# A hybrid attention and recurrence block on one Trainium2 core: the opening in a new order, casts on GpSimd, one output row stored in halves

## The chip, the cores and the metric

The kernel runs on one core of one Trainium2 chip. The metric is the device time of one execution in microseconds (us), as a median over runs. A core has five engines, each with its own in-order queue of instructions: TensorE (PE; its weight loads are shown apart, as PEld), VectorE (DVE), ScalarE (ACT), GpSimd (POOL) and SyncE (SP), which here only issues DMAs. An engine waits at an instruction until what this instruction needs is done, and everything behind it in its queue waits with it.

## The reference, cut to what matters

One decoder layer on x of 1024 tokens by 1024 channels: a conditioned RMSNorm gives h; one large projection gives queries, keys, values, gates and the recurrence's input; windowed attention and a gated linear recurrence follow; two projections are merged, a last projection is gated and added to x, and a final RMSNorm ends it. The change touches only the beginning and the last rows:

```python
mod = c @ w_ada[l] + b_ada[l]
shift, scale, gate = jnp.split(mod, 3, axis=-1)
h = rmsnorm(x, norm_g[l]) * (1.0 + scale[:, None, :]) + shift[:, None, :]
proj = h @ w_in[l]
...
x = x + gate[:, None, :] * (merged @ w_out[l])
return rmsnorm(x, final_g)
```

All is float32. The kernel keeps that precision with products of split operands: each operand is a high part (its value rounded to the matmul's format, `hh` for h and `wh` for a weight) and a low part (the rest, `hl` and `wl`), and a product is the sum of three matmuls, high by high ("h"), low weight by high ("w") and high weight by low ("l").

## The kernel before

**The opening** (to about 68 us) is one hand-written order: a manual schedule fixes, for all five engines, the order in which the code issues instructions.

- `x` comes in eight tiles of 128 tokens (`xt`). For each tile ScalarE squares and sums (`square`), VectorE makes mean and epsilon (`mean`), ScalarE the square root (`root`), and VectorE the reciprocal and the scaling of the tile (`scaled`); for the tiles in `DIAG` VectorE makes only a diagonal matrix, and the scaling happens in the transposition. `flip(i)` transposes tile i on TensorE into four PSUM banks, in two sets that change by pairs of tiles; `out_of(j, p, engine)` evicts bank p of pair j into `xT`, which holds channels by tokens, one row block `kc` (0 to 7) for each 128 channels.
- The condition: `c` is broadcast to all partitions by a matmul (`c_bc`). `modulate(kc)` makes, by two products with accumulation on VectorE, the shift and the scale of the 128 channels of kc from two 512 KB loads of `w_ss`; `scales_of(kc)` finishes them with two small ScalarE instructions. The shift of kc 0 alone comes from a matrix-vector product on TensorE.
- `hi_parts(kc)` makes h's high part on ScalarE (for kc below 4 in two halves of 512 tokens) and then h itself in place (the affine); `lo_parts(kc)` makes the low part on VectorE.
- Four chunks of the large projection are done in the opening (`starts`, numbers 0 to 3). Each chunk's weights come in two halves of 256 KB: half 0 serves kc 0 to 3, half 1 kc 4 to 7. `cast_s(c, i)` makes the high part of half i of chunk c, on ScalarE or GpSimd, and `rest_s(c, i)` the low part on VectorE. `first(kc, terms, chunks)` issues the products of one kc; `chunks(kc)` all three terms, chunk after chunk. There are 192 of them, each 128x128 by 128x512.
- GpSimd also makes the rope angles, a generator of 36 small steps (`angles`), of which `turn(n)` issues the next n. ScalarE's sine (L526) reads the result `trn`; it stands between `chunks(3)` and the shift and scale of kc 5, ahead of the casts of half 1 of chunks 1 to 3.
- Behind this, still in the written order: low parts 5 to 7 and `differences(0)` and `make_operands(0)` on VectorE, and on TensorE `chunks(5)`, then kc 6 and 7 of chunks 0 and 1 (L1605 to L1612).

SP issues all loads of the opening in the order of the code: the tiles of x, the parameters, halves 0 of chunks 2 and 3, `w_ss` for kc 0, halves 0 of chunks 0 and 1, `w_ss` for kc 1 and 2, halves 1 of chunks 0 and 1, and so on.

**The middle** (to about 880 us) runs on TensorE without a pause: Strassen-like products (L709), gates, attention and projections, with the other engines beside them. The change doesn't touch it.

**The end** writes the output in eight rows of 128 tokens by 1024. For rows 6 and 7 the right and the left half are finished by different engines (L1965 by ScalarE, L1969 by VectorE for row 6). Row 6 is stored with one DMA of 512 KB on SP's queue, row 7 with two of 256 KB on SP's and ScalarE's.

Of the kernel before, what the change touches and what calls it, by code (L numbers as in the profile page):

```python
# [12 lines left out]
F32 = mybir.dt.float32  # L13
# [4 lines left out]
AF = mybir.ActivationFunctionType  # L18
ALU = mybir.AluOpType
# [3 lines left out]
P = 128  # L23
S = 1024
D = 1024
# [29 lines left out]
def tile_hybrid_block(ctx, tc, x, pk, rows, posr, posi, c_row, w_ss, w_gate, w_main, w_v,  # L55
# [8 lines left out]
    def f32(ap):  # L64
        return ap.bitcast(F32)
# [24 lines left out]
    def pcol(base, i):  # L90
        return pk_t[:, base + i:base + i + 1]
# [99 lines left out]
    with ExitStack() as st:  # L191
# [14 lines left out]
            xt.append(t)  # L206
        dma(pk_t[:], pk)

        def load_ss(kc):
            for a in (0, 1):  # L210
# [10 lines left out]
        def cast_s(c, i, eng=A):  # L221
            sw[c][i] = slot()
            if eng is G:
                G.tensor_copy(sw[c][i][0][:], raw[c, i])
# [22 lines left out]

        one_row = sp.tile([1, P], F32, name="one_row")
        warm = sp.tile([P, 1], F32, name="warm")
        V.memset(one_row[:], 1.0)  # L250
        zero = rbig[:, :HALF]
        V.memset(zero, 0.0)

# [110 lines left out]
        def square(i):  # L364
            A.activation(junk_t[:].bitcast(BF16), xt[i][:], AF.Square, accum_out=ss[:, i:i + 1])

        def mean(i):
            V.tensor_scalar(out=rr[:, i:i + 1], in0=ss[:, i:i + 1], scalar1=1.0 / D, scalar2=EPS,
                            op0=ALU.mult, op1=ALU.add)

        def root(i):
            A.activation(rr[:, i:i + 1], rr[:, i:i + 1], AF.Sqrt)

        def scaled(i):
            r1 = rr[:, i:i + 1]
            V.reciprocal(r1, r1)
            if i not in DIAG:
                V.tensor_scalar(out=xt[i][:], in0=xt[i][:], scalar1=r1, scalar2=None,
                                op0=ALU.mult)
# [7 lines left out]
        banks = [bk, starts[0] + starts[1]]  # L387

        def flip(i):
            for kc in range(KC):  # L390
                c0 = kc // 4 * 256 + i % 2 * P
                o = banks[i // 2 % 2][kc % 4][:, c0:c0 + P]
                x_ = xt[i][:, kc * P:(kc + 1) * P]
                if i not in DIAG:
                    T.transpose(o, x_, ident[:])
                else:
                    T.matmul(o, x_, dg[i][:], start=True, stop=True)

        def out_of(j, p, eng):
            src = banks[j % 2][p].rearrange("p (a t) -> p a t", a=2)  # L400
            dst = xall[p][:, :, j * 256:(j + 1) * 256]
            if eng is A:
                A.copy(dst, src)
            else:
                V.tensor_copy(dst, src)

        def hi_parts(kc, between=lambda: None):
            kw = dict(scale=gsc[:, kc:kc + 1], bias=shf[:, kc:kc + 1])
            if kc < 4:
                for hf in range(2):  # L410
                    A.activation(hh[kc][hf], xT[kc][:, SL[hf]], AF.Identity, **kw)
            else:
                A.activation(full[kc][0], xT[kc], AF.Identity, **kw)
            between()
            A.activation(xT[kc], xT[kc], AF.Identity, **kw)

        angle = angles()
# [7 lines left out]
        late = {1: [lambda: V.tensor_copy(c_bc[:, SL[0]], psc[0]),  # L425
                    lambda: V.tensor_copy(c_bc[:, SL[1]], psc[1])],
                3: [lambda: out_of(0, 0, V), lambda: out_of(0, 1, V)],
                4: [lambda: out_of(0, 2, V), lambda: out_of(0, 3, A)],
                5: [lambda: out_of(1, 0, V), lambda: out_of(1, 1, V)],
                6: [lambda: out_of(1, 2, A), lambda: out_of(1, 3, A),  # L430
                    lambda: V.scalar_tensor_tensor(
                    out=bng[:], in0=pk_t[:, PK_BSC:PK_BSC + 8], scalar=1.0,
                    in1=pk_t[:, PK_NG:PK_NG + 8], op0=ALU.add, op1=ALU.mult)]}
        for i in range(8):
            square(i)
            mean(i)
            if i:
                root(i - 1)
                scaled(i - 1)
                if i < 6:  # L440
                    turn(3)
                flip(i - 1)
            for f in late.get(i, ()):
                f()
        root(7)
        scaled(7)
        for p in range(4):
            out_of(2, p, A)
        flip(7)
        for k in range(KC):  # L450
            T.matmul(bk[0][:, 0:1], wada[0, 0][:, k * P:(k + 1) * P], pcol(PK_C, k),
                     start=(k == 0), stop=(k == KC - 1))
        for i in range(KEEP_BUSY):
            T.matmul(bk[1], zero[:, 0:P], zero, start=True, stop=True)
# [12 lines left out]
        csn = sp.tile([P, 3, 64], F32, name="csn")  # L467

        def lo_parts(kc):
            if kc < 4:  # L470
                for hf in range(2):
                    V.tensor_tensor(out=hl[kc][hf], in0=xT[kc][:, SL[hf]],
                                    in1=f32(hh[kc][hf]), op=ALU.subtract)
            else:
                V.tensor_tensor(out=full[kc][1], in0=xT[kc], in1=f32(full[kc][0]),
                                op=ALU.subtract)

        def first(kc, terms, cs=range(N_ST)):
            for c in cs:
                h, l = sw[c][kc // 4]  # L480
                c0 = (kc % 4) * P
                for t_ in terms:
                    ww, xh = {"h": (h, hh), "w": (l, hh), "l": (h, hl)}[t_]
                    for hf in range(2):
                        T.matmul(starts[c][hf], ww[:, c0:c0 + P], xh[kc][hf],  # L485
                                 start=(kc == 0 and t_ == "h"), stop=(kc == KC - 1 and t_ == "l"))

# [1 line left out]
            for c in cs:  # L489
                first(kc, terms, (c,))  # L490

        for t_ in "hw":
            first(0, t_, (2, 3, 0))
        scales_of(1)

        def more():
            out_of(3, 2, A)
            out_of(3, 3, A)
        hi_parts(1, more)
        rest_s(1, 0)  # L500
        for t_ in "hw":
            first(1, t_, (2, 3, 0))
        for t_ in "hw":
            for kc in range(2):
                first(kc, t_, (1,))
        lo_parts(0)
# [12 lines left out]
        first(2, "wl")  # L519
        modulate(4)  # L520
        scales_of(4)
# [1431 lines left out]
    def square_d(sl, acc):  # L1953
# [9 lines left out]
    r6 = fs[:, 6, 3:4]  # L1963
    V.reciprocal(r6, fs[:, 6, 2:3])
    A.activation(xo[6][:, RIGHT], xo[6][:, RIGHT], AF.Copy, scale=r6)  # L1965
    gemm(end, A22, wt4, 3, cols=c2)
    add_to(7, c2, end)
    square_d(c2, f[:, 1:2])
    V.scalar_tensor_tensor(out=xo[6][:, LEFT], in0=xo[6][:, LEFT], scalar=r6,  # L1969
                           in1=fg_bc[:, LEFT], op0=ALU.mult, op1=ALU.mult)  # L1970
# [37 lines left out]
def arrange(inputs):  # L2008
# [21 lines left out]
    a["w_ss"][:128] = w_ada[:, :128].reshape(8, 128, 128).transpose(1, 0, 2).reshape(128, 1024)  # L2030
# [26 lines left out]
```

## Time and profile before

| what | value |
|---|---|
| median of 3 runs | 908.18 us (907.96 to 909.19) |
| the profiled execution | 907.33 us |
| its span, first to last instruction | 905.5 us |
| mean granted TensorE clock | 0.998 |
| VectorE, ScalarE, GpSimd busy | 79%, 63%, 13% |
| DMA | 180.74 MB, mean 200 GB/s |

The profiled execution takes 907.33 us, of which 905.5 are the span; 1.8 us lie around it. The median is 0.85 us above it. In the profile's rows, times are us from the span's start. A timeline row gives start, duration, engine, line, operation, what is written and read, how many instructions are merged, and in brackets the idle time before it and what ended it. Line numbers are those of the kernel before; a helper that records an operation gives its own line, so that all DMAs stand at L62.

### The profile page before, as it was taken

Reading aid. Unit: us, or ns where it says so; the run is one execution under the profiler, and the core shown is the slowest. Engines: PE = TensorE matmul, PEld = TensorE weight load, DVE = VectorE, ACT = ScalarE, POOL = GpSimd, SP = SyncE. Lnnn points to the kernel's source line nnn. Section 1 sums busy time; section 2 is a strip of 40 time slices with the busy share of each in tenths; the row PEclk is TensorE's granted clock in tenths of the full one; section 3 lists DMA queues with packets and bytes.
Section 4 is the critical chain, followed back from the end, with each engine's and each line's share of the span. In section 5 each row is a group of like instructions: output and inputs, shape, how many; then the busy total and the mean of one; then the engine's idle time right before and its main releaser. Section 6 shows DMA issues by size and latency. Waiting matters only on the chain.

```text
span 905.5 us, 12663 instructions
## 1 busy us (share of the span) xinstructions
PE 894.3 (99%) x4259; PEld 746.1 (82%) x4259; DVE 718.6 (79%) x1073; ACT 567.2 (63%) x1098; POOL 121.1 (13%) x216
## 2 busy tenths in 40 slices
PE   8999999999999999999999999999999999999996
PEld 6789888888888888888888888888888888888885
DVE  6987688978669875987788597999999847569755
ACT  7965554654566855786585884888888732115435
POOL 6520241200000000000000002343433300000000
PEclk9999999999999999999999999999999999999999
DMA  9828489772435354354446367996656289316504
GB/s 356 338 69 285 165 256 321 256 234 95 151 128 182 121 208 135 124 183 163 158 140 214 105 203 248 349 404 208 215 199 207 74 310 363 140 47 234 207 1 186
DMA packets 87205, 180.74 MB, mean 200 GB/s; under 512 B 8626, under 2 KB 29122, under 8 KB 87140
## 3 DMA queue, kind: packets, MB, share of 16 engines
q1 hardware_dynamic: 83056, 167.07, 52.3%
q0 software_dynamic: 3936, 12.59, 4.3%
q8 instruction: 34, 0.56, 0.3%
q14 instruction: 31, 0.25, 0.1%
q10 hardware_dynamic: 148, 0.27, 0.1%
HBM read 121.34 MB, written 58.95 MB: 199 GB/s over the span
## 4 chain that ended last, share of the span: by engine, by line
PE 93%; DVE 4%; ACT 2%; issue 1%; DVEq 0%; ACTq 0%
PE bk L709 48%; PE rp L173 13%; PE out L1861 6%; PE pmain L173 5%; PE pgate L1025 5%; PE s_ps L1330 3%; PE pv L1403 3%; PE pmain L485 2%; PE bk L485 2%; PE pt L1369 1%; PE pmain L1580 1%; PE pmain L1579 1%; PE pmain L1578 1%; ACT jk L1879 1%; DVE xo L1875 1%
## 5 line engine op out<-in xcount | busy, mean ns | idle before, releaser
L709 PE MATMUL bk<-nh,wh 128*128 128x512 f32 x368 | 143.3, 389 | 0.0
L709 PE MATMUL bk<-nl,wh 128*128 128x512 f32 x368 | 143.2, 389 | 0.0
L709 PE MATMUL bk<-nh,wl 128*128 128x512 f32 x368 | 98.4, 389 | 0.0
L111 DVE TENSOR_TENSOR wl<-r,wh 128x512 fp32r<-128x512 f32 x109 | 75.0, 695 | 24.0 <-ACT wh L105 23.7
L105 ACT CAST wh<-r 128x512 fp32r<-128x512 f32 x107 | 65.5, 618 | 31.0 <-PE rp L173 11.1
L709 PEld LDWEIGHTS bk<-nh,wl 128*128 128x128 f32 x368 | 69.1, 188 | 14.4
L709 PEld LDWEIGHTS bk<-nl,wh 128*128 128x128 f32 x368 | 69.1, 188 | 14.2
L709 PEld LDWEIGHTS bk<-nh,wh 128*128 128x128 f32 x368 | 69.1, 188 | 14.2
L709 PE MATMUL bk<-hl,wh 128*128 128x512 f32 x184 | 71.6, 389 | 0.0
L709 PE MATMUL bk<-hh,wh 128*128 128x512 f32 x184 | 71.6, 389 | 0.0
L111 DVE TENSOR_TENSOR wl<-ws,wh 128x512 fp32r<-128x512 f32 x76 | 52.1, 687 | 7.1 <-ACT wh L105 7.0
L62 POOL DMA_DIRECT2D yh_d<-av x1 | 0.6, 567 | 371.3 <-ACT av L1092 371.3
L1355 ACT ACTIVATE p<-p,small 128x129 f32<-128x129 f32 x128 | 50.0, 396 | 0.0
L709 PE MATMUL bk<-hh,wl 128*128 128x512 f32 x184 | 49.2, 389 | 0.0
L105 ACT CAST wh<-ws 128x512 fp32r<-128x512 f32 x76 | 46.0, 614 | 4.3 <-PE bk L709 2.1
L709 PEld LDWEIGHTS bk<-hh,wl 128*128 128x128 f32 x184 | 34.5, 188 | 7.2
L709 PEld LDWEIGHTS bk<-hl,wh 128*128 128x128 f32 x184 | 34.6, 188 | 7.1
L709 PEld LDWEIGHTS bk<-hh,wh 128*128 128x128 f32 x184 | 34.5, 188 | 7.1
L1330 PEld LDWEIGHTS s_ps<-ks,qs 128*128 128x128 f32 x256 | 34.4, 189 | 3.7 <-DVE p L1345 1.1
L1330 PE MATMUL s_ps<-ks,qs 128*128 128x256 f32 (+1 forms) x256 | 35.3, 280 | 0.6 <-DVE p L1345 0.6
L709 PE MATMUL bk<-hha,wh 128*128 128x512 f32 x92 | 35.8, 389 | 0.0
L709 PE MATMUL bk<-hla,wh 128*128 128x512 f32 x92 | 35.8, 389 | 0.0
(378 smaller groups left out, 2289.3 us busy)
## 6 DMA issues: line engine op xcount, KB each, us to landing
r<-w_main SPq DMA_DIRECT2D x100, 256.0 KB, 4.2
wada<-w_ss SPq DMA_DIRECT2D x16, 512.0 KB, 9.0
qs<-q_d SPq DMA_DIRECT2D x16, 512.0 KB, 4.9
wo_d<-wr SPq DMA_DIRECT2D x28, 256.0 KB, 3.0
wo<-wo_d SPq DMA_DIRECT2D x14, 512.0 KB, 5.1
ks<-k_d SPq DMA_DIRECT2D x12, 384.0 KB, 4.3
xt<-x SPq DMA_DIRECT2D x8, 512.0 KB, 7.0
sma_d<-c SPq DMA_DIRECT2D x16, 256.0 KB, 4.4
```

Source lines behind the costliest of these rows:

```text
L105: A.copy(dst[0][:], src)
L111: V.tensor_tensor(out=dst[1][:], in0=src, in1=f32(dst[0][:]), op=ALU.subtract)
L173: mm = T.matmul(ps[hf], ww, xx[kc][hf], start=(kc == 0 and ww is w_h and xx is xh), stop=(kc == KC - 1 and xx is xl))
L485: T.matmul(starts[c][hf], ww[:, c0:c0 + P], xh[kc][hf], start=(kc == 0 and t_ == "h"), stop=(kc == KC - 1 and t_ == "l"))
L709: W["pe"] = T.matmul(ps, ww[:, kc * P:(kc + 1) * P], b[kc][i], start=(first and n == 0), stop=(n == 11), skip_group_check=not first)
L1025: W["pe"] = T.matmul(ps[:, SL[hf]], ww[:, c0:c0 + P], xx_[:, SL[hf]], start=(ic == 0 and i == 0), stop=(ic == 1 and i == 2))
L1330: W["pe"] = T.matmul(o, qs[:, j, qc], ks[:, kb:n % 2 + 2, b, :], start=(b == 0), stop=(b == 1))
L1355: A.activation(px[:, j, :], px[:, j, :], AF.Exp, bias=sm[:, 0, j:j + 1], accum_out=sm[:, 1, j:j + 1])
L1369: W["pe"] = T.transpose(pt[:, j, :], px[:, j, 0:P], ident[:])
L1403: W["pe"] = T.matmul(pv[:], b, m[:].rearrange("p j q -> p (j q)"), start=(i == 0), stop=(i == len(prods) - 1))
L1578: T.matmul(o, hh[kc][th][:, ts_], wh[:, cols], start=(kc == 0), stop=False)
L1861: T.matmul(o, a[k][x_][:, p * P:(p + 1) * P], b[k][y_][:, cols], start=(first and k == 0 and i == 0), stop=(k == 3 and i == 2), skip_group ...
```

## The change

It reorders the opening and splits one store:

- The mean goes into the root: one ScalarE square root with scale 1/D and the epsilon as bias, from the sum of squares; the eight VectorE instructions of `mean` are gone. `DIAG` is 0 and 2 only, so tile 4 is scaled by VectorE. `flip` goes through the kc in the order 0, 4, 1, 5, ..., and tile 5 is flipped twice.
- The matrix-vector product of kc 0 goes; its shift is made by `modulate(0, (0,))` on VectorE, and its `w_ss` half is loaded ahead of the weights of chunks 2 and 3.
- GpSimd makes `bng` and five casts (half 0 of all four chunks, and half 1 of chunk 0, which ScalarE made later), after 17 steps of the angles, and the other 19 steps after them.
- The first products are made by halves of the tokens, over all four chunks; the high-part products of kc 0 and 1 come ahead of their low parts.
- Row 6's right half is stored as soon as it is ready, the left half after it.

```diff
-DIAG = 0, 2, 4
+DIAG = 0, 2
...
+        load_ss(0, (0,))
         for c in (2, 3):
             load_s(c, 0)
-        load_ss(0)
+        load_ss(0, (1,))
...
-            A.activation(shf[:, kc:kc + 1], mods[:, kc:kc + 1] if kc else bk[0][:, 0:1],
-                         AF.Identity, bias=pcol(PK_BSH, kc))
+            A.activation(shf[:, kc:kc + 1], mods[:, kc:kc + 1], AF.Identity,
+                         bias=pcol(PK_BSH, kc))
...
-        def mean(i):
-            V.tensor_scalar(out=rr[:, i:i + 1], in0=ss[:, i:i + 1], scalar1=1.0 / D, scalar2=EPS,
-                            op0=ALU.mult, op1=ALU.add)
         def root(i):
-            A.activation(rr[:, i:i + 1], rr[:, i:i + 1], AF.Sqrt)
+            A.activation(rr[:, i:i + 1], ss[:, i:i + 1], AF.Sqrt, scale=1.0 / D, bias=eps[:])
...
+        norm(0, 1)
+        scaled(0)
+        scaled(1)
+        for hf in range(2):
+            V.tensor_copy(c_bc[:, SL[hf]], psc[hf])
+        flip(0)
+        flip(1)
+        norm(2, 3, 4)
+        scaled(2)
+        scaled(3)
+        evict(0, v=(0, 1, 2), a=(3,))
+        turn(14)
+        flip(2)
+        flip(3)
+        scaled(4)
+        norm(5)
+        evict(1, a=(3,))
+        norm(6)
+        scaled(5)
+        flip(4)
+        flip(5)
+        flip(5)
+        modulate(0, (0,))
+        scaled(6)
+        norm(7)
+        evict(1, v=(0, 1), a=(2,))
         scaled(7)
-        for p in range(4):
-            out_of(2, p, A)
+        evict(2, a=(0, 2, 3, 1))
+        flip(6)
         flip(7)
-        for k in range(KC):
-            T.matmul(bk[0][:, 0:1], wada[0, 0][:, k * P:(k + 1) * P], pcol(PK_C, k),
-                     start=(k == 0), stop=(k == KC - 1))
...
-        for c in (2, 3):
+        for c in (2, 3, 0, 1):
             cast_s(c, 0, G)
-        cast_s(0, 0)
+        cast_s(0, 1, G)
         turn()
         modulate(0, (1,))
-        for p in range(2):
-            out_of(3, p, A)
         scales_of(0)
-        hi_parts(0, lambda: cast_s(1, 0))
-        for c in (2, 3, 0):
-            rest_s(c, 0)
-        modulate(1)
+        rest_s(2, 0)
+        rest_s(3, 0)
...
+        hi_half(0, 0)
+        first(0, "hw", (2, 3), (0,))
+        evict(3, a=(0,), v=(2,))
+        affine_half(0, 0)
+        rest_s(0, 0)
+        rest_s(1, 0)
+        modulate(1, (0,))
+        first(0, "h", (0, 1), (0,))
+        hi_half(0, 1)
+        lo_half(0, 0)
+        modulate(1, (1,))
+        first(0, "h", (2, 3), (1,))
+        first(0, "w", (0, 1), (0,))
+        first(0, "w", (2, 3), (1,))
+        evict(3, a=(1, 3))
+        affine_half(0, 1)
+        first(0, "hw", (0, 1), (1,))
+        first(0, "l", (2, 3, 0, 1), (0,))
         scales_of(1)
...
+        hi_parts(1)
+        lo_half(0, 1)
+        for hf in range(2):
+            first(1, "hw", (2, 3, 0, 1), (hf,))
+        first(0, "l", (2, 3, 0, 1), (1,))
         modulate(2)
         scales_of(2)
         hi_parts(2)
         lo_parts(1)
-        first(0, "l")
         first(1, "l")
         first(2, "h")
         modulate(3)
         scales_of(3)
         hi_parts(3)
         lo_parts(2)
-        cast_s(0, 1)
         first(2, "wl")
...
     A.activation(xo[6][:, RIGHT], xo[6][:, RIGHT], AF.Copy, scale=r6)
+    dma(out[6 * P:7 * P, RIGHT], xo[6][:, RIGHT])
...
-    dma(out[6 * P:7 * P, :], xo[6][:])
+    dma(out[6 * P:7 * P, LEFT], xo[6][:, LEFT])
```

New helpers: `norm` is `square` and `root` of each tile named; `evict(j, a, v)` calls `out_of` for the banks in `a` on ScalarE and then for those in `v` on VectorE; `hi_half`, `affine_half` and `lo_half` are one half (512 tokens) of `hi_parts` and `lo_parts`.

More of the change, by code (lines that the diff above doesn't have):

```diff
@@ L207, in tile_hybrid_block, with load_ss @@
         dma(pk_t[:], pk)
-        def load_ss(kc):
-            for a in (0, 1):
+        def load_ss(kc, which=(0, 1)):
+            for a in which:
                 wa_t = sp.tile([P, D], F32, tag="xt", name="wada", bufs=XT)
@@ L389, in flip @@
         def flip(i):
-            for kc in range(KC):
+            for kc in (0, 4, 1, 5, 2, 6, 3, 7):
                 c0 = kc // 4 * 256 + i % 2 * P
@@ L434, in tile_hybrid_block, with norm, evict @@
[L434 to L445, printed above, removed]
+        def norm(*tiles):
+            for i in tiles:
+                square(i)
+                root(i)
+        def evict(j, **by):
+            for eng, ps in ((A, by.get("a", ())), (V, by.get("v", ()))):
+                for p in ps:
+                    out_of(j, p, eng)
@@ L466, in tile_hybrid_block, with hi_half, affine_half, lo_half @@
-        modulate(1)
+        rest_s(2, 0)
+        rest_s(3, 0)
+        def hi_half(kc, hf):
+            A.activation(hh[kc][hf], xT[kc][:, SL[hf]], AF.Identity, scale=gsc[:, kc:kc + 1],
+                         bias=shf[:, kc:kc + 1])
+        def affine_half(kc, hf):
+            x_ = xT[kc][:, SL[hf]]
+            A.activation(x_, x_, AF.Identity, scale=gsc[:, kc:kc + 1], bias=shf[:, kc:kc + 1])
         csn = sp.tile([P, 3, 64], F32, name="csn")
+        def lo_half(kc, hf):
+            V.tensor_tensor(out=hl[kc][hf], in0=xT[kc][:, SL[hf]], in1=f32(hh[kc][hf]),
+                            op=ALU.subtract)
@@ L471, in lo_parts @@
                 for hf in range(2):
-                    V.tensor_tensor(out=hl[kc][hf], in0=xT[kc][:, SL[hf]],
-                                    in1=f32(hh[kc][hf]), op=ALU.subtract)
+                    lo_half(kc, hf)
             else:
@@ L476, in lo_parts, with first @@
                                 op=ALU.subtract)
-        def first(kc, terms, cs=range(N_ST)):
+        def first(kc, terms, cs=range(N_ST), halves=range(2)):
             for c in cs:
@@ L483, in first @@
                     ww, xh = {"h": (h, hh), "w": (l, hh), "l": (h, hl)}[t_]
-                    for hf in range(2):
+                    for hf in halves:
                         T.matmul(starts[c][hf], ww[:, c0:c0 + P], xh[kc][hf],
```

33 lines of the change are left out of this document (7 added, 26 removed).

## The prediction

> **What bounds the kernel now.** I read the page first, then the waits of PE, then the timelines of the first 70 us engine by engine, and last the end of the span.
>
> ```profile
> span 905.5 us, 12663 instructions
> PE 894.3 (99%) x4259; PEld 746.1 (82%) x4259; DVE 718.6 (79%) x1073; ACT 567.2 (63%) x1098; POOL 121.1 (13%) x216
> PE bk L485 <- ACT hha L411: 0.8, 2, 0.7
> PE s_ps L1330 <- DVE p L1345: 0.6, 1, 0.6
> PE bk L485 <- ACT hhb L411: 0.2, 1, 0.2
> ```
>
> The page says that TensorE is busy for 99% of the span, and PE's waits (total, times, longest) say that after the opening it hardly waits at all. So a time that PE loses or wins in the first 70 us goes through to the end almost one for one.
>
> ```profile
> 23.44 0.47 PE L485 MATMUL bk<-hha,wh 128*128 128x512 f32 x1 [0.68 <-ACT hha L411]
> 27.73 0.50 PE L485 MATMUL bk<-hhb,wh 128*128 128x512 f32 x1 [0.20 <-ACT hhb L411]
> 48.04 0.62 PE L485 MATMUL pmain<-hh,wh 128*128 128x512 f32 x2
> 59.83 0.61 PE L485 MATMUL pmain<-hl,wh 128*128 128x512 f32 x2
> 57.72 5.44 PE pmain L485 x24
> ```
>
> PE's timeline: the four-chunk products start at 23.44 and run without a gap from 27.73. The last row, from the chain that ended last, prices one product at 5.44/24 = 0.227 us. By the order in the code, the product at 48.04 is the first of chunk 1 with kc 4 and needs the cast of that chunk's second half; the one at 59.83 is the first with the low part of kc 7.
>
> **What is moved, and what it costs: GpSimd.** The change puts five weight casts into GpSimd's queue, the fifth being the second half of chunk 0, `cast_s(0, 1, G)`, and behind them `turn()`, the rest of the rope angles. Before, that fifth cast was ScalarE's:
>
> ```profile
> 37.04 0.61 ACT L105 CAST wh<-r 128x512 fp32r<-128x512 f32 x1
> 17.09 1.62 SPq L62 DMA_DIRECT2D r<-w_main  x2
> r<-w_main SPq DMA_DIRECT2D x1, 256.0 KB, 9.8
> 15.17 1.28 POOL L224 CAST wh<-r 128x512 fp32r<-128x512 f32 x2 [0.57 <-DMA r<-w_main]
> 20.45 0.78 POOL L291 TENSOR_SCALAR ra<-sa 128x64 f32<-128x64 f32 x1
> 31.97 1.03 POOL L356 TENSOR_SCALAR trn<-trn 128x128 f32<-128x128 f32 x1
> ```
>
> Its data, r(0,1), are issued at 17.09 and take 9.8 us to land (the third row is the DMA view of that one issue), so they are there at 26.9. The reordering of the loads doesn't change this: one 512 KB load passes two of 256 KB, and every byte ahead of r(0,1) is the same. GpSimd is in order. Its other casts (0.61 us each, from 1.28/2) end soon after their loads, by about 20.3; then it stands still until 26.9, where before it was working through the angles. The generator has 36 steps. Before, 18 were done ahead of the casts, the other 18 ran from the casts' end at 16.45 to 33.00, so 0.92 us each. After, 3 + 14 = 17 are done early and **19 stand behind the fifth cast**.
>
> How long do 19 take? Alone such a step is short, beside VectorE it is not:
>
> ```profile
> 7.40 0.32 POOL L297 TENSOR_TENSOR a<-ang,t 128x64 f32<-128x64 f32 x1
> 22.56 1.28 POOL L291 TENSOR_SCALAR rt<-tt 128x64 f32<-128x64 f32 x1
> 22.22 1.34 DVE L275 SCALAR_TENSOR_TENSOR jk<-wada,c_bc 128x1024 bf16<-128x1024 f32 x1
> 44.03 1.22 DVE L275 SCALAR_TENSOR_TENSOR jk<-wada,c_bc 128x1024 bf16<-128x1024 f32 x1
> L275 DVE SCALAR_TENSOR_TENSOR jk<-wada,c_bc 128x1024 bf16<-128x1024 f32 x10 | 12.4, 1242 | 0.2
> L472 DVE TENSOR_TENSOR hlb<-xT,hhb 128x512 fp32r<-128x512 f32 x3 | 2.3, 774 | 0.0
> L472 DVE TENSOR_TENSOR hla<-xT,hha 128x512 fp32r<-128x512 f32 x3 | 2.1, 688 | 0.1
> L111 DVE TENSOR_TENSOR wl<-r,wh 128x512 fp32r<-128x512 f32 x3 | 2.0, 689 | 0.9 <-ACT wh L105 0.9
> L475 DVE TENSOR_TENSOR hl<-xT,hh 128x1024 fp32r<-128x1024 f32 x1 | 1.2, 1220 | 0.0
> ```
>
> The step at 22.56 ends at 23.84, just behind VectorE's product (22.22 to 23.56). From 20.45 to 33.00 GpSimd makes 13 steps, and VectorE about as many operations: it lets one step in between two of its own. The last five rows are VectorE's groups from 28 to 47 us, 20 operations in 19 us, of the kind that will run there after the change too. The fifth cast, against a running product, ends near 28.4. At the old 0.92 us, 19 steps end at 28.4 + 17.5 = 45.9. At one step per operation they end with the 19th operation behind the cast, the second product of kc 6; that one ended at 45.25 (the row at 44.03). After the change VectorE is some 2 us later there, since modulate(2) can start near 29.0 where it started at 27.04, and a step of GpSimd beside it costs most operations about 0.1 us (1.34 against 1.22): 48.6. Both ends stay in the range; I take **48.0**, nearer the second, since the stretch past 39 us has more long products.
>
> The Trainium skill, page "SBUF — State Buffer", section "Who interferes with whom", says that a VectorE instruction with two SBUF inputs and a GpSimd one that reads SBUF exclude each other, the later one waiting for the whole of the earlier. By that rule the sum takes the later end, 48.6, rather than 45.9; the rows above agree with it (1.28 us beside the product, 0.32 without).
>
> **Who waits for the angles.** ScalarE's sine reads them, and a queue stands behind it:
>
> ```profile
> 40.70 1.28 ACT L526 ACT_TABLE_LOAD   x1
> 41.99 0.31 ACT L526 ACTIVATE csn<-trn 128x128 f32<-128x128 f32 x1
> 45.52 1.65 ACT L105 CAST wh<-r 128x512 fp32r<-128x512 f32 x3
> 46.16 1.90 DVE L111 TENSOR_TENSOR wl<-r,wh 128x512 fp32r<-128x512 f32 x3 [0.90 <-ACT wh L105]
> 57.83 1.22 DVE L475 TENSOR_TENSOR hl<-xT,hh 128x1024 fp32r<-128x1024 f32 x1
> ```
>
> Before, the angles were there 9 us ahead of the sine at 41.99. Behind it on ScalarE: the sine's copy, scale and shift of kc 5, its high part and affine, and the casts of chunks 1 to 3, whose first starts 45.52 - 41.99 = 3.53 us after the sine. VectorE's rests wait for those casts (46.16), and behind them stand the low parts of kc 5 to 7; the last ends at 59.05, 12.89 us after 46.16. PE needs it at 59.83, so this line has 0.78 us to spare now. After: sine at 48.0, first cast at 51.6, rests from 52.2, low part of kc 7 at 65.1. PE, waiting first near 48 for the cast of chunk 1 (about 4 us) and again for that low part (under 1 us), does the old 59.83 product at 65.1: **+5.3 us**. Put as a rule: PE loses (end of the angles - 42.7) us. With 45.9 it is +3.2, with 48.6 +5.9. The opening's own saving doesn't soften this, since the line doesn't run through PE.
>
> **The front.** Off: the 16 matvec passes on PE, three ScalarE casts (37.04's 0.61 us each), eight means on VectorE, one diagonal flip, `bng`. On: modulate(0, shift) on VectorE (1.24 us), a full scaling for tile 4, one more eviction by VectorE, a flip of tile 5 made twice as filler. The root that takes over the mean stays one short instruction on ScalarE, which waits for tiles of x in that stage anyway: nothing. `bng` goes to GpSimd's idle time ahead of the casts: nothing, unless the casts were waited for. On SP one load changes places with two and no issue is added here.
>
> ```profile
> 20.04 1.84 PE L451 MATMUL bk<-pk_t,wada 128*128 128x1 f32 x16
> 23.73 1.23 DVE L275 SCALAR_TENSOR_TENSOR jk<-wada,c_bc 128x1024 bf16<-128x1024 f32 x1 [0.16 <-DMA wada<-w_ss]
> 18.27 0.75 DVE L378 TENSOR_SCALAR xt<-xt,rr 128x1024 f32<-128x1024 f32 x1
> 13.35 0.68 DVE L405 COPY xT<-bk 128x512 f32<-128x512 f32 x1
> ```
>
> VectorE is what paces the new order. From about 15.7 (w_ss(0) lands some 0.6 us after the 15.17 at which GpSimd got the half as large r(2,0) in the same place; scaling 5 is done too): product 1.26, scaling 6 0.9, two evictions 1.2, scaling 7 0.9, product 1.2, and about 0.8 behind GpSimd's casts: 22.0. ScalarE then makes the scale and the first high half, and PE starts near **23.0** (23.44 before). Then two rests, one eviction, two rests, product, low half, product: 6.1 us more, so modulate(1) ends at 28.1, where it ended at 24.96 before. PE has 20 products done by then and waits until 29.3 for kc 1; before, at 29.3, it had done 13 + (29.3 - 27.73)/0.227 = 20. So the new opening wins **nothing** (bounds: 0.9 won if GpSimd costs VectorE nothing; 0.5 lost if it costs twice that). What ends last there is VectorE's product of kc 1, no longer ScalarE.
>
> **The end.** Row 6 goes out in halves.
>
> ```profile
> 898.70 0.72 ACT L1965 ACTIVATE xo<-xo,rbig 128x512 f32<-128x512 f32 x1 [0.23 <-DVE rbig L1964]
> 899.37 0.75 DVE L1969 SCALAR_TENSOR_TENSOR xo<-xo,rbig,fg_bc 128x512 f32<-128x512 f32 x1
> 900.00:900.80 0.80, 0.00 (x0) 0.00 (x0) 0.76 (x3) 0.57 (x1) 0.00 (x0) 1.00 0.00 0
> 902.40:903.20 0.80, 0.00 (x0) 0.00 (x0) 0.00 (x0) 0.00 (x0) 0.00 (x0) 0.71 0.99 394
> ```
>
> The right half is ready at 899.42, the left at 900.12; the DMA engines move nothing until 900.8 (last two columns: share, GB/s), then rows 6 and 7 at up to 394. Half a row, 0.262 MB, takes 0.67 us at that rate and can now go in the idle 0.7 us; SP's one issue more is made while SP waits for the left half: **-0.65** (between 0, if the last landing is bound by latency, and -0.7).
>
> **The sum:** +5.3 - 0.65 = +4.65 us on the profiled execution's 907.33, and 908.18 + 4.65 = **912.8** on the median (the execution lies 0.85 below it). With the bounds +3.2 and +5.9 and the tail's 0: 910.7 to 914.1.
>
> **The rivals.** (1) GpSimd is through in time, and the time doesn't rise. It decides at 42.7: 19 steps in 14.3 us, 0.75 each. For it: alone they take 0.32 to 0.45, and VectorE may have more gaps than I think. Against it: 0.92 before, with the same neighbour. Then only the tail and the front are left: 0 to -0.9 and -0.65, about **907.5**. (2) As (1), and the front also wins more than an us, because products and scalings run free of GpSimd from 20.3 to 26.9: **906.2**. (3) PE's clock falls in the long gap. At the start, after idling, 12 small products take 4.55 us, later four take 1.02, while the granted clock reads 1.00 throughout:
>
> ```profile
> 1.38 4.55 PE L256 MATMUL bk<-rbig 128*128 128x512 bf16 x12 [1.38 <-DVE warm L258]
> 21.74 1.02 PE L454 MATMUL bk<-rbig 128*128 128x512 bf16 x4
> ```
>
> That is 4.55 - 12 x 0.255 = 1.5 us lost. If a gap of 4 us brings this back, the time is 912.8 + 1.5 = **914.3**, partly taken back by the second wait, which shrinks. No gap of that length stands in the trace of before. The Trainium skill, page "TensorE: Matmul & The Clock Gate", section "What's actually happening", speaks of half clock after an idle window of some 3.4 us; by that rule a gap just above it can fall either way.
>
> **Chances.** Forecast 0.60, clock 0.13, in time 0.18, front wins 0.07, others 0.02. A measurement of this kernel can tell about 0.2%, 1.8 us, from no change. Faster 0.08, same 0.18 (906.4 to 910.0), slower 0.74. The forecast's own range is 910.2 to 914.5; to leave out no more than 2 in 10 it has to take in rival (1) and the clock: 907.3 to 915.2.
>
> **What would show it.** After: GpSimd's fifth cast waits for a DMA from about 20 to 26.9; the last `trn` step ends at 46 to 49; ScalarE's sine waits for POOL some 4 us; PE has one gap of 3 to 5 us near 48 before a chunk 1 product with kc 4, released by the cast, and one under 1 us near 65; modulate(1) ends near 28. If `trn` ends before 43, the forecast is wrong and rival (1) holds; if the gap is there but kc 4's products are spaced over 0.3 us, rival (3).

## The result, and the profile after

| | before | after |
|---|---|---|
| median | 908.07 us (6 runs, 907.62 to 909.19) | 912.58 us (6 runs, 910.82 to 913.71) |
| ratio of after to before, 95% interval | | 1.0051 [1.0041, 1.0061] |
| the profiled execution | 907.33 us | 910.82 us |

The changed kernel is 4.5 us slower; 912.8 was forecast. The two profiled executions differ by 3.5 us only: 3.2 in the span and 0.3 around it (1.8 us before, 2.1 after). The rest is taken up further down. First the page of the kernel after:

```profile
span 908.7 us, 12629 instructions
PE 893.3 (98%) x4242; PEld 743.8 (82%) x4243; DVE 720.4 (79%) x1068; ACT 567.2 (62%) x1095; POOL 126.6 (14%) x221
```

Its view of TensorE's waits (total, times, longest, in us):

```profile
PE pmain L394 <- DVE xT L404: 1.5, 1, 1.5
PE pmain L506 <- ACT wh L105: 1.4, 1, 1.4
...
PE s_ps L1358 <- DVE p L1373: 0.9, 2, 0.7
PE bk L506 <- ACT hha L410: 0.7, 1, 0.7
PE pmain L506 <- DVE hl L496: 0.5, 1, 0.5
...
PE pmain L1606 <- DVE c L645: 0.2, 1, 0.2
```

TensorE is busy for 1 us less than before, and the span is 3.2 us longer: the time is lost in waits. The first row is new too, but it stands ahead of the products, in the transpositions (at 18.99), and the first four-chunk product comes no later for it: 23.07 against 23.44. Behind 30 us three waits of the opening are new: for a weight cast (`wh`), for a low part (`hl`), for a rotated piece of chunk 0 (`c`). The timeline of the kernel after shows where they stand and who made them:

```profile
23.07 0.47 PE L506 MATMUL bk<-hha,wh 128*128 128x512 f32 x1 [1.01 <-ACT hha L478]
29.30 0.50 PE L506 MATMUL bk<-hha,wh 128*128 128x512 f32 x1 [0.67 <-ACT hha L410]
46.70 0.62 PE L506 MATMUL pmain<-hh,wh 128*128 128x512 f32 x2
49.61 0.73 PE L506 MATMUL pmain<-hh,wh 128*128 128x512 f32 x2 [1.39 <-ACT wh L105]
62.54 0.73 PE L506 MATMUL pmain<-hl,wh 128*128 128x512 f32 x2 [0.53 <-DVE hl L496]
71.62 0.36 PE L1606 MATMUL pmain<-wh,hha 128*128 128x256 f32 x1 [0.16 <-DVE c L645]
...
25.64 0.62 POOL L224 CAST wh<-r 128x512 fp32r<-128x512 f32 x1 [5.13 <-DMA r<-w_main]
26.34 0.69 POOL L325 TENSOR_SCALAR tmp<-t 128x64 f32<-128x64 f32 x1
44.37 1.03 POOL L359 TENSOR_SCALAR trn<-trn 128x128 f32<-128x128 f32 x1
...
42.05 1.28 ACT L554 ACT_TABLE_LOAD   x1
45.43 0.31 ACT L554 ACTIVATE csn<-trn 128x128 f32<-128x128 f32 x1 [2.10 <-POOL trn L359]
48.96 1.64 ACT L105 CAST wh<-r 128x512 fp32r<-128x512 f32 x3
...
26.72 1.25 DVE L278 SCALAR_TENSOR_TENSOR jk<-wada,c_bc 128x1024 bf16<-128x1024 f32 x1
28.62 1.25 DVE L278 SCALAR_TENSOR_TENSOR jk<-wada,c_bc 128x1024 bf16<-128x1024 f32 x1
49.59 1.90 DVE L111 TENSOR_TENSOR wl<-r,wh 128x512 fp32r<-128x512 f32 x3 [2.08 <-ACT wh L105]
61.27 1.22 DVE L496 TENSOR_TENSOR hl<-xT,hh 128x1024 fp32r<-128x1024 f32 x1
```

Read it from the middle. GpSimd stands for 5.13 us in front of the fifth cast, which waits for its load. Its 19 steps follow, from 26.34 to 45.40, 1.00 us each. ScalarE has loaded the sine's table at 43.33 and waits 2.10 us for `trn`. The casts start 3.53 us behind the sine, as before, VectorE waits 2.08 us for them, and TensorE meets two holes: chunk 1 of kc 4 starts at 49.61, where 48.04 stood before, and the low part of kc 7 at 62.54, where 59.83 stood: +1.57 and then +2.71 us. At 46.70 TensorE was still where the kernel before had it (46.68, the same product in that timeline). The first product of v, next in the timelines of before and after:

```profile
68.44 0.28 PE L1578 MATMUL pmain<-wh,hha 128*128 128x256 f32 x1
```

It comes at 71.62 instead of 68.44, +3.18 us; a further 0.55 comes in at the start of the attention (the wait for `p`), and 0.5 is won at the very end. Sum: 3.2 us of span.

### The profile page after: what moved, and what is told of

It is laid out like the page before. It is cut to its first block, busy times and chain, and to the rows that moved or that the text cites. A ratio compares the mean times of both kernels' runs of the same rounds, so it can differ in the third digit from the quotient of the medians.

```text
span 908.7 us, 12629 instructions
## 1 busy us (share of the span) xinstructions
PE 893.3 (98%) x4242; PEld 743.8 (82%) x4243; DVE 720.4 (79%) x1068; ACT 567.2 (62%) x1095; POOL 126.6 (14%) x221
## 4 chain that ended last, share of the span: by engine, by line
issue 43%; PE 41%; DVE 6%; DMA 4%; ACT 2%; POOL 2%; SPq 0%; DVEq 0%; ACTq 0%; POOLq 0%
PE rp L173 14%; PE bk L737 7%; PE out L1889 6%; PE pmain L173 5%; PE s_ps L1358 3%; PE pv L1431 3%; DMA r<-w_main 2%; PE pt L1397 1%; DMA yl_d<-it 1%; PE pmain L1606 1%; PE pmain L1608 1%; PE pmain L1607 1%; DMA xt<-x 1%; DMA wr<-w_gate 1%; ACT jk L1907 1%
## 5 line engine op out<-in xcount | busy, mean ns | idle before, releaser
L105 ACT CAST wh<-r 128x512 fp32r<-128x512 f32 x104 | 63.6, 617 | 30.3 <-PE rp L173 11.1
```

Of the source, the lines that this page charges most:

```text
L105: A.copy(dst[0][:], src)
```

## The experiments

There are twelve runs, e1 to e13 without an e11; e6 is the changed kernel itself. Medians are compared with runs of the kernel before on the same chip, 907.61 to 908.17 us in the median of each set.

| run | median | ratio to before, 95% interval |
|---|---|---|
| e1, cast back on ScalarE | 909.04 us | 1.0018 [1.0009, 1.0026] |
| e2, cast on GpSimd behind the angles | 908.91 us | 1.0015 [1.0006, 1.0024] |
| e3, before, with that cast ahead of the angles | 911.67 us | 1.0043 [1.0031, 1.0056] |
| e4, before, with the split store | 907.33 us | 0.9994 [0.9985, 1.0003] |
| e5, after, sine behind the casts | 909.11 us | 1.0014 [1.0006, 1.0023] |
| e6, after once more | 912.03 us | 1.0055 [1.0042, 1.0068] |
| e7, e1 with the sine behind the casts | 908.89 us | 1.0008 [1.0000, 1.0017] |
| e8, e1 with the shift of kc 0 on TensorE | 908.95 us | 1.0018 [1.0006, 1.0031] |
| e9, after, with the load issued earlier | 909.13 us | 1.0016 [1.0007, 1.0025] |
| e10, e1 with the low part of kc 7 earlier | 909.18 us | 1.0019 [1.0010, 1.0028] |
| e12, e4 with the mean in the root | 907.42 us | 0.9996 [0.9987, 1.0005] |
| e13, before, products of kc 2 made twice | 909.46 us | 1.0023 [1.0012, 1.0034] |

### Is it the cast that waits ahead of the angles? (e1, e2, e3, e9, e5)

e1 undoes one line of the change, e2 only moves it, e3 makes it alone in the kernel before:

```diff
# e1, on the kernel after
-        cast_s(0, 1, G)
         turn()
...
         lo_parts(2)
+        cast_s(0, 1)
# e2, on the kernel after
-        cast_s(0, 1, G)
         turn()
+        cast_s(0, 1, G)
# e3, on the kernel before
+        cast_s(0, 1, G)
...
-        cast_s(0, 1)
```

> The changed kernel with the second-half cast of chunk 0 back on ScalarE, behind the low part of kc 2. Theory (the cast's wait for its load holds up the angles, the sine, the later casts and so TensorE): GpSimd no longer waits at 25.6, the 19 steps start near 20.5 and end near 40, before ScalarE reaches the sine at 43.3; TensorE has no wait near 48 and no more than 0.9 us near 60; what is left of the change is the front (within 0.5 us of nothing) and the split store (-0.5): 907.0 to 908.3 us. Rival (the loss comes from the new front itself, or from VectorE being slowed by the casts of half 0): the time stays above 910.

> The changed kernel with that cast still on GpSimd, but behind the 19 steps of the angles instead of ahead of them. Theory: the cast comes near 40, its low part is made on VectorE near 41 and needed by TensorE near 47, the sine doesn't wait: within 0.6 us of the kernel with the cast on ScalarE, 907.0 to 908.5. Rival (it is the cast's work on GpSimd that costs, by keeping VectorE off the memory port): it stays over 1 us above that kernel.

> The kernel before with one edit: the second-half cast of chunk 0 moved from ScalarE into GpSimd's queue ahead of the last 18 steps of the angles. Theory: the cast waits for its load until 26.9 and ends near 27.5, 18 steps of 1.0 us end near 45.6, and by the rule of the prediction (loss = end of the angles - 42.7) TensorE loses 2.9 us: 910.3 to 911.8. Rival (the loss belongs to the new front): within 0.5 us of the kernel before.

In e1 and e2 the last step of the angles (L359) ends at 37.57 and 38.35, nobody waits for `trn`, and TensorE's wait for the casts is gone. From the timeline of e1, the last step and the two waits of TensorE's that are left behind 48 us:

```profile
36.54 1.03 POOL L359 TENSOR_SCALAR trn<-trn 128x128 f32<-128x128 f32 x1
...
59.84 0.73 PE L505 MATMUL pmain<-hl,wh 128*128 128x512 f32 x2 [0.55 <-DVE hl L495]
68.92 0.35 PE L1606 MATMUL pmain<-wh,hha 128*128 128x256 f32 x1 [0.17 <-DVE c L645]
```

e2 makes the same cast on the same engine and is as fast as e1: it isn't the work of the cast that costs, but its place. Both are slower than expected, though (909.04 and 908.91, where at most 908.3 and 908.5 were expected); the next section is about that. e3 brings the stall into the kernel before (timeline):

```profile
25.92 0.79 POOL L224 CAST wh<-r 128x512 fp32r<-128x512 f32 x1 [9.97 <-DMA r<-w_main]
44.14 1.03 POOL L356 TENSOR_SCALAR trn<-trn 128x128 f32<-128x128 f32 x1
...
45.21 0.31 ACT L526 ACTIVATE csn<-trn 128x128 f32<-128x128 f32 x1 [3.32 <-POOL trn L356]
...
49.39 0.73 PE L486 MATMUL pmain<-hh,wh 128*128 128x512 f32 x2 [1.35 <-ACT wh L105]
62.33 0.73 PE L486 MATMUL pmain<-hl,wh 128*128 128x512 f32 x2 [0.56 <-DVE hl L476]
71.42 0.36 PE L1578 MATMUL pmain<-wh,hha 128*128 128x256 f32 x1 [0.18 <-DVE c L617]
```

One moved line makes the whole chain of the kernel after: the same waits, the first product of v at +2.98 us, the median at +0.43%. The two runs that follow attack the chain at its other links: e9 lets the data come earlier, and e5 takes away who waits.

```diff
# e9, on the kernel after
+        load_s(0, 1)
         load_ss(1)
         load_ss(2)
-        load_s(0, 1)
# e5, on the kernel after
         chunks(3)
-        (sine, its negated copy and their stores)
...
         for c in range(1, N_ST):
             cast_s(c, 1)
             rest_s(c, 1)
+        (sine, its negated copy and their stores)
```

> Changed kernel, all casts and steps where they are, but the load of the second half of chunk 0 is issued ahead of the loads of w_ss(1) and w_ss(2) instead of behind them (2 MB earlier, about 5 us at the 400 GB/s of that stretch). Theory (GpSimd loses its 5 us standing in front of a cast whose data aren't there): the cast starts at about 20.5 us without a wait, the angles end near 40 to 41 us, the sine doesn't wait, TensorE's wait of 1.4 us for the casts of chunks 1 to 3 goes, and the time is that of the runs without a stall, 908.5 to 909.5 us. Rival (w_ss(1) then lands too late for the product of kc 1 on VectorE, which is due at 24.5 us): the stall goes, but TensorE waits 0.6 us or more longer for kc 1, and the time is 909.6 to 910.5 us.

> Changed kernel, but the sine, its negated copy and its stores are issued behind the casts and rests of chunks 1 to 3 instead of ahead of them; the cast of the second half of chunk 0 stays on GpSimd ahead of the angles. Theory (the angles are late, and cost time only because ScalarE's queue stands behind the sine): GpSimd ends its angles near 45.4 us as in the changed kernel, the casts start near 44 to 45 us instead of 48.96, TensorE's wait for the casts is gone, and the time is that of the two runs without a stall or a little less, 907.3 to 909.3 us. Rival (GpSimd's work of 26 to 45 us itself slows VectorE, or the new front costs the time): 911 us or more.

e9's timeline, then e5's:

```profile
20.75 1.14 POOL L224 CAST wh<-r 128x512 fp32r<-128x512 f32 x1 [1.02 <-DMA r<-w_main]
39.20 0.53 POOL L359 TENSOR_SCALAR trn<-trn 128x128 f32<-128x128 f32 x1
...
42.91 0.31 ACT L554 ACTIVATE csn<-trn 128x128 f32<-128x128 f32 x1
```

```profile
44.86 1.03 POOL L359 TENSOR_SCALAR trn<-trn 128x128 f32<-128x128 f32 x1
...
45.75 1.64 ACT L105 CAST wh<-r 128x512 fp32r<-128x512 f32 x3
47.41 1.28 ACT L562 ACT_TABLE_LOAD   x1
48.71 0.31 ACT L562 ACTIVATE csn<-trn 128x128 f32<-128x128 f32 x1
```

In e9 the cast waits 1.02 instead of 5.13 us, and the sine no longer waits; its rival is there in small, the wait for kc 1 is 0.9 instead of 0.7 us. In e5 the angles are as late as after the change (45.89), but the casts don't stand behind them any more. Both take 909.1 us, as e1 and e2 do. Four different cuts, one time: the stall is the wait of the cast, handed on through GpSimd's queue, the sine and ScalarE's queue, and it costs 912.0 to 912.6 less 909.0, so 3.0 to 3.6 us. e5's rival, that GpSimd's late work costs the time by slowing VectorE, falls: its angles are as late as after the change, and its median is e1's.

### Why do these four take 909 us, and not less than before? (e4, e12, e6)

Without the stall the forecast was about 907.5, and the expectation of e1 was like it; all four come out about 1.5 us above. Is the split store to blame? e4 makes it alone in the kernel before:

```diff
+    dma(out[6 * P:7 * P, RIGHT], xo[6][:, RIGHT])
...
-    dma(out[6 * P:7 * P, :], xo[6][:])
+    dma(out[6 * P:7 * P, LEFT], xo[6][:, LEFT])
```

> The kernel before with row 6 stored in halves and nothing else. Theory: the right half moves in the idle 0.7 us ahead of the left one: 0.4 to 0.7 us faster, 907.4 to 907.7. Rival (the last landing is bound by latency): no difference.

e4's ratio of 0.9994 can't be told from 1. Its span shows the gain nevertheless: from VectorE's last operation on row 6 (899.37 before, 900.45 in e4, 903.10 after) to the span's end (905.5, 906.1, 908.7) it is 6.1 us before and 5.6 in both others. The left half of row 6 in the timeline of the kernel after, then two of its windows (columns: window, length, busy time of PE, PEld, DVE, ACT and POOL, PEclk, DMA share, GB/s):

```profile
903.10 0.75 DVE L1998 SCALAR_TENSOR_TENSOR xo<-xo,rbig,fg_bc 128x512 f32<-128x512 f32 x1
...
903.20:904.00 0.80, 0.00 (x0) 0.00 (x0) 0.76 (x3) 0.33 (x2) 0.00 (x0) 1.00 0.00 0
904.00:904.80 0.80, 0.00 (x0) 0.00 (x0) 0.72 (x1) 0.68 (x1) 0.00 (x0) 1.00 0.92 353
```

The left half of row 6 is ready at 903.85, and from 904.0 on the DMA engines move data, some 0.2 us later; before, nothing moved until 900.8, 0.7 us behind the left half (900.12).

> Kernel before with two edits of the change alone: row 6 stored in halves (907.33 in its own run) and the mean inside the root, which takes eight short operations and a hop between ScalarE and VectorE out of the opening. Theory (VectorE and the hop pace the scalings of the old opening): the first four-chunk product starts 0.2 to 0.5 us earlier, time 906.8 to 907.2 us, the fastest of all. Rival (loads and ScalarE's squares pace them): no change of the opening, 907.2 to 907.7 us.

The mean in the root, the change's other clean part, leaves the old opening as it was: the first product starts at 23.60 in e12, and at 23.29 to 23.94 in the four other profiles of the old opening. The time is the rival's; that loads and squares are what paces this opening is not shown by it.

> The changed kernel once more, on the chip of the next three runs, for a second profile. Theory (the late angles cost all of the loss): about 912.6 us, the end of the angles between 45.0 and 46.0 us, one wait of TensorE of about 1.4 us for a cast of chunks 1 to 3 and one of about 0.5 us for the low part of kc 7. Rival (the surplus of the median over the profiled execution comes from the angles ending later in other executions): the end of the angles moves by more than 1 us between the two profiles, and the time of the profiled execution with it.

The second profile repeats the first: the last step ends at 45.23 (45.40), TensorE's waits are 1.4 and 0.6, the profiled execution takes 910.19 us. So between these two the angles don't wander. That doesn't rule the rival of e6 out, since in both sets the profiled execution is the fastest, 1.8 us below its median, while it is 0.7 below in the kernel before (907.33, 908.07). What the slower executions of the changed kernel lose in addition stands in no trace here; they lose it within their spans (910.0 to 911.6 us, against 908.7).

### The front wins, and VectorE gives it back (e7, e8, e10, e13)

What the runs without a stall lose in the opening can be read from two rows each. Counted from the first four-chunk product, the first product of v comes 45.00, 45.23 and 45.51 us later in the three profiles of the old front without added work (before, e12, e4), and 46.4 to 46.8 in the seven of the new front without the stall: 1.4 us more in the mean. The new front starts its products at 22.75 in the mean of nine profiles against 23.55 in five with the old front. So 0.8 us are won there, and 1.4 are lost behind it.

The candidate was the queue that ends with the low part of kc 7, since TensorE waits 0.55 us for it in e1. It runs over ScalarE and VectorE. e7 relieves ScalarE of the sine, e8 VectorE of one product:

```diff
# e7, on e1: the sine behind the casts, as in e5
# e8, on e1
-        modulate(0, (0,))
...
+        for k in range(KC):
+            T.matmul(bk[0][:, 0:1], wada[0, 0][:, k * P:(k + 1) * P], pcol(PK_C, k),
+                     start=(k == 0), stop=(k == KC - 1))
```

> Changed kernel with the cast of the second half of chunk 0 back on ScalarE (as in the first run, 909.04) and the sine behind the casts of chunks 1 to 3. Theory (without the stall the new front still loses what it won, because the queue of ScalarE and VectorE that ends with the low part of kc 7 has only 0.8 us to spare): taking the sine, its copy and its table load out of that queue brings the low part of kc 7 at least 1 us earlier, TensorE's wait of 0.5 us for it goes, and the time falls by 0.5 to 1.2 us against the first run: 907.8 to 908.6 us. Rival (the front's loss sits ahead of 30 us or behind 70 us): the wait goes, and the time stays within 0.3 us of 909.0.

> Changed kernel with the cast of the second half of chunk 0 back on ScalarE, and the shift of kc 0 made by 16 passes on TensorE again instead of the product on VectorE (1.24 us). Theory (VectorE paces the new front and all of the line behind it): first product and the low part of kc 7 come 0.6 to 1.2 us earlier, time 908.0 to 908.6 us. Rival (loads or ScalarE pace the front): within 0.3 us of the first run's 909.0, or slower by the passes' 0.5 us or so.

Both theories missed. In e7 the casts start 0.7 us earlier than in e1, counted from the first product (46.27 - 22.91 against 46.26 - 22.21), and still the low part of kc 7 ends 37.5 us behind it, where e1 has 37.6. The wait for `hl` stays at 0.6 us, and the median stays too; its ratio is lower than e1's, but the intervals overlap. In e8 the VectorE time taken out ahead of 19 us was idle time in part, VectorE waits 0.82 us for ScalarE at 27.68 instead, and neither the first product (23.06) nor the median improves. What the two traces do show is VectorE's own line: from 19 to 60 us it hardly stops but for ScalarE's casts (0.90 us before, 0.68 in e1), and it begins the products of kc 2 later. In the timelines of the kernel before, of the kernel after and of e1:

```profile
27.04 1.34 DVE L275 SCALAR_TENSOR_TENSOR jk<-wada,c_bc 128x1024 bf16<-128x1024 f32 x1
...
28.62 1.25 DVE L278 SCALAR_TENSOR_TENSOR jk<-wada,c_bc 128x1024 bf16<-128x1024 f32 x1
...
27.75 1.25 DVE L278 SCALAR_TENSOR_TENSOR jk<-wada,c_bc 128x1024 bf16<-128x1024 f32 x1
```

Against the first product that is 3.60 us before and 5.55 and 5.54 in the two others, 1.9 us more; the low part of kc 7 had 0.78 us to spare. e10 takes the wait for this low part away, and e13 delays VectorE in front of kc 2 in the kernel before, by 2.5 us of added work, where nothing else is changed:

```diff
# e10, on e1
     differences(0)
+    lo_parts(7)
     make_operands(0)
     chunks(5)
-    lo_parts(7)
# e13, on the kernel before
         modulate(2)
+        modulate(2)
```

> Changed kernel with the cast of the second half of chunk 0 on ScalarE (the first run, 909.04), and in VectorE's queue the low part of kc 7 ahead of the two operands nl of 2.4 us instead of behind them. Theory (what the new front wins ahead of 30 us is lost because VectorE, which works without a gap from 19 to 60 us, comes 0.7 to 1.4 us later to the low part of kc 7 than before; it isn't ScalarE's queue, as the run with the sine moved showed): TensorE's wait of 0.5 to 0.6 us for that low part goes, the first of the following products comes 0.5 to 0.7 us earlier, and the time is 908.0 to 908.5 us. Rival (the next wait, that of the products of v for the rotated chunk 0, takes it back): the wait for hl goes, that for c grows from 0.2 to 0.7 us, and the time stays at 909.0.

> Kernel before with the two products of kc 2 on VectorE made twice, 2.5 us more of VectorE in front of kc 2 and nothing else. Theory (the line of VectorE from there to the low part of kc 7 is what the opening ends on, with only 0.78 us to spare in the kernel before, so a front that hands it over later loses the surplus, even where TensorE starts earlier): TensorE, without a wait there before, waits near 60 us, 1.7 us in all for the low part of kc 7 and for what stands ahead of it, the first product of v comes 1.7 to 2.2 us later against the first four-chunk product, and the time is 909.3 to 910.0 us. Rival (VectorE's own waits, 0.90 us for the casts among them, take the surplus up): less than 0.8 us, 908.4 us at most.

One of TensorE's waits in e10, and then its timeline in e13:

```profile
PE pmain L1606 <- DVE c L645: 0.9, 1, 0.9
```

```profile
23.50 0.47 PE L485 MATMUL bk<-hha,wh 128*128 128x512 f32 x1 [0.68 <-ACT hha L411]
...
48.52 0.73 PE L485 MATMUL pmain<-hh,wh 128*128 128x512 f32 x2 [0.22 <-ACT wh L105]
61.45 0.73 PE L485 MATMUL pmain<-hl,wh 128*128 128x512 f32 x2 [0.57 <-DVE hl L475]
70.53 0.36 PE L1579 MATMUL pmain<-wh,hha 128*128 128x256 f32 x1 [0.17 <-DVE c L618]
```

In e10 the wait for `hl` is gone, and that for `c`, 9 us further down VectorE's queue, grows from 0.2 to 0.9: its rival held, and the time is e1's. In e13 2.5 us of VectorE work bring the kernel before the two waits of e1, with a third for a cast: the low part of kc 7 is used 1.62 us later than at 59.83, the first product of v comes 47.03 us behind the first four-chunk product (+2.03), and the median rises by 0.23%, to 909.46. The theory held, but for the sum of the listed waits (1.7 us expected, 0.96 found; the last section says why). So in this opening VectorE's line is a second bound close behind TensorE's, with two due points; moving one of them only shows the other.

The opening so explains some 0.6 us (1.4 less 0.8) of the 1.5. Two more places show in the records. One lies at 566 us, at the start of the attention: its third group of scores (`s_ps`) waits for VectorE to be done with `p`. The timelines of the kernel before, then of e1:

```profile
546.38 1.23 DVE L1089 TENSOR_TENSOR rz<-rz,th 128x1024 f32<-128x1024 f32 x1 [0.33 <-DMA th<-sgr_d]
561.65 0.69 DVE L1350 TENSOR_REDUCE small<-p 128x4 f32<-128x516 f32 x1 [5.09 <-DMA yl_d<-it]
565.13 1.11 PE L1330 MATMUL s_ps<-ks,qs 128*128 128x256 f32 x8
...
548.00 1.23 DVE L1117 TENSOR_TENSOR rz<-rz,th 128x1024 f32<-128x1024 f32 x1 [1.24 <-DMA th<-sgr_d]
563.38 0.69 DVE L1378 TENSOR_REDUCE small<-p 128x4 f32<-128x516 f32 x1 [5.21 <-DMA yl_d<-it]
566.57 1.22 PE L1358 MATMUL s_ps<-ks,qs 128*128 128x256 f32 x8 [0.56 <-DVE p L1373]
```

VectorE stands behind two transfers there, the load of `th` and the store `yl_d`. From the first product of v (68.44 and 68.92) to its next operation behind the store it takes 1.25 us longer in e1. TensorE's wait is 0.56, 0.29, 0.60 and 0.31 us in e1, e2, e5 and e9, and its products fall back by 0.5 to 0.9 us. Of the five profiles of the old front only e12 has this wait, with 0.18; with the new front e6 and e8 lack it. (A wait of 0.6 to 0.7 us for `p` near 605 us stands in every profile.) Why the load of `th` comes later stays open; no run was made on it. The other place lies outside the span: of the executions whose span is on record, every one of the old front and of e8 has 1.7 to 1.9 us there, every other one of the new front 2.0 to 2.1, so some 0.3 us more. No view shows what fills it. No version beats the kernel before: the intervals of e4 and e12 take in no change.

## Why the prediction was right, point by point

- **What bounds: right.** The 3.18 us lost ahead of the first product of v are still there at the end of the span.
- **The stall: the right mechanism, mis-sized.** The fifth cast on GpSimd does wait for its load, the 19 steps stand behind it, the sine waits for them, and TensorE has two holes, near 48 and in the sixties. The rule "PE loses (end of the angles - 42.7) us" holds to the digit at the product it was made for: 45.40 - 42.7 = 2.70, and the row at 62.54 is 2.71 later than 59.83. The term that was off is the cast's end: 28.4 forecast, 26.26 measured. The forecast took the 9.8 us that this load had needed once; after, it took 8.7 (the row of the DMA view is at the end of this document), and the cast took 0.62 us instead of 1.5. The steps were right: 1.00 us each, between the 0.92 and 1.06 of the two bounds. But the end of the angles, 45.4, fell 0.5 us below the lower bound of 45.9, since both bounds shared the same cast. The stall so came to 2.7 us on that line, not 5.3, and the loss near 48 to 1.57 us instead of 4. Of the signs that the prediction lists, the order and the releasers came as written, and three sizes came out smaller: the end of the angles (45.4, not 46 to 49), the sine's wait (2.10, not 4) and TensorE's gap (1.39, not 3 to 5).
- **GpSimd beside VectorE.** The Trainium skill, page "SBUF — State Buffer", section "Who interferes with whom", would have its steps wait for whole VectorE operations. This trace agrees in the main: a step takes 1.00 us on average, where 0.32 stood without a neighbour. The sum by that rule, 48.6, was 3.2 us too late; 2.1 are the cast's end, 1.1 the steps, which took a little less than the 1.06 us that it gave them.
- **The front: each time right, the conclusion wrong.** Forecast were a first product at 23.0, modulate(1) done at 28.1 and kc 1 at 29.3; measured were 23.07, 27.97 and 29.30, and at 46.70 TensorE stood where it had stood before. That the opening therefore "wins nothing" is the step that failed: the text has VectorE "some 2 us later there" and uses it only to price GpSimd's steps. The same delay reaches the low part of kc 7, whose spare time of 0.78 us the text names one paragraph on. By e1, e2, e5 and e9 the kernel without the stall takes 909.0 us, where rival (1) had 907.5, so the rest of the change costs about 1.5 us more than forecast. VectorE's later hand-over is shown for some 0.6 of it; the wait at 566 us and the 0.3 us outside the span are the rest, and their cause is open. In the kernel after, the stall and the later hand-over meet on one line, so that they don't add up in full.
- **The end:** -0.65 forecast, -0.5 in the spans.
- **The sum** of +4.65 met the median's +4.5 with a stall that was sized too large, a front that was taken to cost nothing, and a rest of about one us between the profiled executions (+3.5) and the medians that no trace shows. The number is better than its working.
- **The rivals.** (1) needed the angles by 42.7 and got them at 45.4. (2) needed the same; its front did win 0.8 us at the first product, and lost it again. (3) wasn't put to the test: TensorE's longest wait behind the first product is 1.39 us, far from 4, the granted clock is 1.00 in the windows around it, and only the first pairs behind it are longer (0.73 against 0.62 us).

## What to carry to other kernels

A piece of work moved to an idle engine takes its waits along: place it where its data are there, or behind the work that others wait for, since in an in-order queue its wait becomes everyone's. When a front is reordered, work out for each engine, not only for the one that is busiest, when it hands over to what follows, and compare that with the spare time of each due point further down. A bound shared by both ends of a range (here one landing time) makes the range too narrow.

## What the runs showed that was not expected

The view of DMA issues of the kernel after, for the load of half 1 of chunk 0, issued at 16.93 (the count, the size, the us to landing):

```profile
r<-w_main SPq DMA_DIRECT2D x1, 256.0 KB, 8.7
```

The same load landed after 9.8 us in the kernel before, issued at 17.09, with the same bytes ahead of it. In the thirteen profiles that issue it in this place (all but e9's) it takes 8.5 to 9.8 us; the forecast rested on the longest.

The fifth cast took 0.62 us at 25.64, although VectorE's queue ran on there. VectorE seems to have paid instead; its row in the kernel after:

```profile
25.67 1.12 DVE L488 TENSOR_TENSOR hla<-xT,hha 128x512 fp32r<-128x512 f32 x1
```

This operation, begun just behind the cast, took 1.12 us; the same one took 0.71 in e1, where GpSimd has no cast at that point, and in e3 the operation begun during the cast took 1.10. Where the cast stands elsewhere it took up to 1.39 us (e2).

The wait list understates a stall: in e13 the new waits add up to 0.96 us, and the first product of v is 2.03 us late. The ends of matmuls are modelled, and the starts tell more: at 48.52 the wait is listed with 0.22 us, and by the fourth product TensorE is 0.81 us behind the kernel before (both counted from the first four-chunk product), since the pairs behind a gap take 0.73 us instead of 0.62 and start further apart.
